# Moving query projections, statistics, roots and the meta rows in a hybrid encoder layer

## The chip, the cores and the metric

The kernel runs on one core of a Trainium2 chip. Such a core has five engines, each with a queue of its own that it works through in order: TensorE (PE in the rows: matrix products and transposes into PSUM banks; PEld is its weight load), VectorE (DVE), ScalarE (ACT), GpSimd (POOL) and SyncE (SP, which here issues the DMA transfers). The metric is the device time of one execution in microseconds, as the median of three runs.

## The reference, cut to what matters

```python
def encoder_layer(h, ...):
    u = rms_norm(h, pre_g)                       # 16 meta rows + 512 or 1024 tokens, 1024 wide
    z = u @ w_in                                 # 1024 x 7168
    c_val, c_glu, c_gate, q, k, v, a_gate = split(z)
    conv_out = conv_module(c_val, c_glu, ...) * silu(c_gate)
    att = neighbourhood_attention(q, k, v, ...) * silu(a_gate)
    y = concatenate([conv_out, att]) @ w_out
    return h + rms_norm(y, post_g)

def conv_module(val, glu_gate, conv_w, conv_b, ln_g, ln_b):
    u = val * sigmoid(glu_gate)
    y = depthwise_conv(u, conv_w) + conv_b       # 31 taps
    return silu(layer_norm(y, ln_g, ln_b))
```

Attention has 16 heads of 64; each query sees a window of 8 rows by 16 columns of a grid 64 wide, with a relative bias, and the 16 meta tokens. Prompt and samples share the meta tokens, so that all 16 + 512 + 1024 columns go through one program.

## The kernel before

All projections are computed nearly in full precision by splitting each fp32 operand into a high part of type f32r and an f32r rest. A product is then three f32r products: high by high, high by low, low by high. `split_w` (L140) makes the two parts of a weight: ScalarE copies the high part, and VectorE or GpSimd subtracts it from the raw weight. `proj` (L175) is one projection tile: 8 slices of 128 rows by 3 products, 24 in all, of up to 512 columns.

The program has four parts.

1. **Start**, 0 to about 36 us. `prenorm(s)` normalizes tile `s` (0 is the 16 meta rows, 1 to 12 are 128 tokens each), transposes it and splits it into `uh` and `ul`. The loop at L363 takes them in the order 1, 0, 2, 3, ... and puts the first units of `v_units` (24 products of 256 columns, one for each token tile) between them. `load_v(0)` loads and splits the first quarter of the value weights into `vh` and `vl`; its low part is made by VectorE, those of later quarters by GpSimd. At step `IVM` the value products of the meta rows are issued (`v_meta`, with the small fp32 product with `sel`, L305).
2. **Convolution**, to about 640 us: projections on TensorE beside 31 taps for each channel block on VectorE. The results go to DRAM (`zs`).
3. **Attention**, about 648 to 1163 us: 8 pairs of heads, each with 3 groups of queries in 2 halves, 48 steps in all. A step `n` of the loop at L682 issues the scores of half `n` (`scores`: 4 tiles `ss`, each three f32r products, then the maximum on VectorE, L584, the exponential on ScalarE, and a scaling), the weighted sums of half `n-2` (`weighted`, L615, plain fp32), the transposes of half `n-1` (`transposes`, L599, and ScalarE's copy `pT`, L601), and two kinds of filling work:
   - `between(p, i)`, with `i` from 0 to 5 within a pair: the query projections `pair_q` (its own groups 1 and 2 at `i` 0 and 2, the next pair's group 0 at `i` 5) and the four key projections of the next pair (two at `i` 1, one each at 3 and 4). `pair_q` ends in four copies `qh` on ScalarE and four subtractions `ql` on VectorE, `pair_proj` in `kh` and `kl`.
   - one step of the generator `statistics`: layer-norm moments of the convolution's result, read back from `zs`. For each of 12 token tiles it loads two half tiles, sums over the channel blocks on VectorE (L659, into `ms`, a part of the tile `cw_sb`), sums over the partitions by an fp32 product with `ones` on TensorE (L663), and stores the row to `std`; then the same for the squared deviations. These are 24 `ones` products. Its last two steps (L671 to L676) read all variances back, take the root on ScalarE and the reciprocal on VectorE, and store the result.
4. **Output**, about 1196 us to the end: `mix(t)` builds one token tile (L763 to L770: subtract the mean, multiply, Silu, multiply with the gate, split) and `product` multiplies it with the output weights (L790). The first tile's convolution part, `mix(0, (0,))`, is placed behind the last transposes copy and ahead of the weight loads `load_wo`. The last two gate projections (`a_gate(6, 7)`) run on TensorE from 1163 to 1196 us.

PSUM has three banks for projections and `ones` products, two for scores, two for transposes and one for weighted sums. Three query buffers are used in turn, one for a half.

The order of the source is not the final order. A scheduler of the framework orders each engine's queue when the program is built, and it may bring an instruction forward past others if its inputs allow. `tc.issue_after(x)` holds the instructions of its block that run on the engine of `x` behind `x`; `last_qk`, `last_mm`, `last_pv` and `last_pt` are the latest score product, projection product, weighted sum and transposes copy.

Of the kernel before, what the change touches and what calls it, by code (L numbers as in the profile page):

```python
# [16 lines left out]
DC = 8  # L17
# [25 lines left out]
NVS = 7  # L43
NXT = 4
LAG = 1
IVM = 3
TAP_US = 2.3
STAT0 = 3
STEP_US = dict(v=2.8, c=5.5, a=5.5)
# [44 lines left out]
def tile_encoder(ctx: ExitStack, tc: tile.TileContext, mt, xn, w_main, w_v, wo, cw, cb, lg, lb, pg, postg, rbt, rmask, y):  # L94
    nc = tc.nc
# [77 lines left out]
    last_mm = [None]  # L173
# [112 lines left out]
    def load_v(qv):  # L286
        raws, his, los = [], [], []
        for half in range(2):
            raws.append(wpool.tile([128, 4, 256], F32, name="wraw", tag="wraw", bufs=2))
            nc.sync.dma_start(raws[half], w_v[qv][:, half * 4:half * 4 + 4])  # L290
            his.append(vpool.tile([128, 4, 256], F32R, name="vh", bufs=2))
            los.append(vpool.tile([128, 4, 256], F32R, name="vl", bufs=2))
            split_w(raws[half], his[half], los[half], nc.vector if qv == 0 else nc.gpsimd)
        return raws, his, los

    def v_meta(qv, raws):
# [16 lines left out]
    def v_units():  # L313
        for qv in range(4):
            _, vh, vl = vws.pop(qv)
            for t in range(12):
                ps = new_mm()
                uh, ul = u_cols(16 + 128 * t, 16 + 128 * t + 128)
                for dc in range(DC):
                    for i, (u, w) in enumerate(((uh, vh), (uh, vl), (ul, vh))):  # L320
                        nc.tensor.matmul(ps[:, :256], lhsT=u[dc // 4][:, dc % 4, :], rhs=w[dc // 4][:, dc % 4, :],  # L321
                                         start=(dc == 0 and i == 0), stop=(dc == DC - 1 and i == 2))
                vs = vpool.tile([128, 256], F32, name="vs", bufs=3)
                nc.scalar.copy(out=vs, in_=ps[:, :256])  # L324
                row = (ROW_P, ROW_A, ROW_B)[t // 4]
                for i in range(2):
                    nc.sync.dma_start(vd[(t % 4) * 2 + i, row * 8:row * 8 + 64, qv * 256:qv * 256 + 256], vs[i * 64:i * 64 + 64])
                if t == 11 and qv < 3:
                    vws[qv + 1] = load_v(qv + 1)
                    metas.append(qv + 1)  # L330
                yield
# [28 lines left out]
        nc.gpsimd.tensor_tensor(out=sel, in0=sel, in1=ident[:, j:j + 16], op=ALU.add)  # L360
    with tc.tile_pool(name="start", bufs=2, side="right", reuse_waits="tile") as sp:
        gb = sp.tile([128, D], F32, name="gb", bufs=1)
        for i, s in enumerate((1, 0) + tuple(range(2, 13))):  # L363
            prenorm(s, sp, gb)
            if i == 0:
                vws[0] = load_v(0)
                vraw0 = vws[0][0]
            if i == IVM:
                v_meta(0, vraw0)
            if LAG <= i < LAG + NVS:  # L370
                next(vfill)
            if s == 5:
                ahead[8] = load_w(8)
                ahead[0] = load_w(0)
        for dst, src in ((cw_sb[:, :, :KW], cw), (cb_sb, cb), (lg_sb, lg), (lb_sb, lb), (rm_sb, rmask)):
            nc.sync.dma_start(dst, src)
# [36 lines left out]
    for c in range(8):  # L413
        if c > 0:
            z = new_z()
        steps = convolve(c, z)
# [65 lines left out]
    last_qk = [None]  # L482
# [145 lines left out]
    def between(p, i):  # L628

        if i in (0, 2):  # L630
            pair_q(p, i // 2 + 1)
        elif p == NPAIR - 1:
            for _ in range(1 if i == 1 else 2):
                next(rest)
        elif i == 5:
            pair_q(p + 1, 0)
        else:
            if i == 1:
                knext[0] = pair_proj(p + 1)
                next(knext[0])  # L640
            next(knext[0])
# [5 lines left out]
    def statistics():  # L647
        for t in range(TG // 128):
# [8 lines left out]
            for moment in range(2):  # L657
                for x, sl in hx:
                    nc.vector.tensor_reduce(out=ms[:, sl], in_=x.rearrange("p c t -> p t c"), op=ALU.add, axis=mybir.AxisListType.X)  # L659
                yield  # L660
                ps = new_mm()
                with tc.issue_after(last_qk[0].ins):
                    nc.tensor.matmul(ps[:, :128], lhsT=ones, rhs=ms, start=True, stop=True)  # L663
                nc.scalar.copy(out=row[0:1], in_=ps[0:1, :128])
                nc.sync.dma_start(std[moment:moment + 1, tsl], row[0:1])
                if moment == 0:
                    for x, sl in hx:
                        nc.vector.tensor_tensor(out=x, in0=x, in1=ps[:, sl].unsqueeze(1).broadcast_to([128, 8, 64]), op=ALU.subtract)
                        nc.scalar.activation(out=x, in_=x, func=AF.Square)
        yield  # L670
        s = std[1:2]  # L671
        var = bass.AP(s.tensor, s.offset, [[1, 128], [128, TG // 128]])
        nc.sync.dma_start(rv, var)
        nc.scalar.activation(out=rv, in_=rv, func=AF.Sqrt, bias=eps_sb[:, 1:2])
        nc.vector.reciprocal(rv, rv)
        nc.sync.dma_start(var, rv)  # L676
        yield

    stats = statistics()
    knext, last_pv, last_pt = [None], [None], [None]  # L680
# [2 lines left out]
    for n in range(len(groups) + 2):  # L683
        if n < len(groups):
            p, g, hf = groups[n]
# [9 lines left out]
            next(rest)  # L695
        if 0 <= n - 1 < len(groups):
            transposes(*groups[n - 1])
        if n >= STAT0:
            next(stats, None)
        if n < len(groups):  # L700
            between(p, g * 2 + hf)
    with tc.issue_after(last_pv[0]):
        for _ in a_gate(6, 7):
            pass
# [65 lines left out]
            (nc.vector if t < MLT else nc.gpsimd).tensor_tensor(out=ml, in0=mx, in1=mh.bitcast(F32), op=ALU.subtract)  # L770

    with tc.issue_after(last_pt[0]):
        mix(0, (0,))
    for n in range(16):
        if n == 6:
# [132 lines left out]
```

## Time and profile before

| | before |
|---|---|
| median of 3 runs | 1474.44 us (1472.86 to 1474.65) |
| the profiled execution | 1473.84 us, of which 1471.8 us are its span (first to last instruction) |
| TensorE busy | 1442.7 us, 98% of the span |
| VectorE, ScalarE, GpSimd busy | 1012.5, 559.5, 250.2 us |
| share of TensorE in the chain that ended last | 86% |

An engine is busy while it executes an instruction; waiting for a semaphore is idle time. "The chain that ended last" follows the program back from its last instruction to whatever released each step. In the rows, an instruction's length includes the time it takes to pass through the engine, and the next one starts before it ends; the pace of products is therefore read from start to start. A bracket at a row's end gives the idle time just before it and what ended that. A line such as L495 is that of the kernel before; after the change, lines beyond L317 are one or two higher.

### The profile page before, as it was taken

The numbers are of one execution on the slowest core, as the hardware profiler recorded it, in microseconds if no ns is written. First come the engines' busy times: TensorE is split into PE (matmuls) and PEld (weight loads), VectorE is DVE, ScalarE is ACT, GpSimd is POOL, SyncE is SP. The second block draws the span as 40 slices with busy tenths as digits, with TensorE's granted clock in tenths as the row PEclk, the third lists the DMA queues.
The fourth block names the chain that finished last, engine by engine and source line by source line (L and its number), as shares of the span: only waits on it lengthen the run. The fifth ranks groups of instructions, "written<-read, shape, count | busy, mean of one in ns | idle before, by whom it ended". The sixth has DMA issues, their size and how long they took to land.

```text
span 1471.8 us, 24149 instructions
## 1 busy us (share of the span) xinstructions
PE 1442.7 (98%) x9536; PEld 1237.9 (84%) x9536; DVE 1012.5 (69%) x1741; ACT 559.5 (38%) x1299; POOL 250.2 (17%) x186
## 2 busy tenths in 40 slices
PE   7999999999999999999999999999999999999998
PEld 6988998988998888888888888888878878888886
DVE  6599999998999899846767676666654174432421
ACT  7312111112111111235545555455544475554440
POOL 2042022112101211222111121111110102122120
PEclk9999999999999999999999999999999999999999
DMA  8113113312231212343132232322232495644531
GB/s 272 35 47 114 50 55 110 93 40 88 82 91 50 99 48 87 108 101 102 43 94 79 76 93 59 102 79 77 46 101 74 150 304 148 173 132 137 159 106 43
DMA packets 153465, 145.21 MB, mean 99 GB/s; under 512 B 37216, under 2 KB 125432, under 8 KB 153352
## 3 DMA queue, kind: packets, MB, share of 16 engines
q1 hardware_dynamic: 153352, 143.67, 32.7%
q8 instruction: 75, 1.23, 0.3%
q14 instruction: 38, 0.31, 0.1%
HBM read 105.35 MB, written 42.72 MB: 101 GB/s over the span
## 4 chain that ended last, share of the span: by engine, by line
PE 86%; issue 4%; DMA 4%; DVE 2%; ACT 2%; POOL 1%; SPq 0%; DVEq 0%; POOLq 0%; ACTq 0%
PE mm L180 35%; PE py L790 17%; PE tp L180 9%; PE ss L577 5%; PE po L180 5%; PE po L615 4%; PE mm L321 3%; PE tp L599 3%; PE tp L321 3%; DMA wraw<-in_w_main 1%; DMA wraw<-in_wo 1%; POOL vl L142 1%; PE po L321 1%; PE mm L663 1%; DMA wraw<-in_w_v 1%
## 5 line engine op out<-in xcount | busy, mean ns | idle before, releaser
L180 PE MATMUL mm<-uw,whi 128*128 128x512 f32 (+2 forms) x1904 | 566.3, 372 | 0.0
L272 DVE SCALAR_TENSOR_TENSOR z<-ub,cw_sb,z 128x1536 f32<-128x1536 f32 (+2 forms) x270 | 497.4, 1849 | 8.1
L180 PEld LDWEIGHTS mm<-uw,whi 128*128 128x128 f32 x1904 | 343.7, 188 | 56.9 <-issue 1.3
L180 PE MATMUL mm<-uw,wlo 128*128 128x512 f32 (+2 forms) x952 | 353.3, 371 | 1.1 <-POOL wlo L142 1.1
L142 POOL TENSOR_TENSOR wlo<-wraw,whi 128x1024 fp32r<-128x1024 f32 x48 | 130.5, 2719 | 627.7 <-ACT whi L141 618.5
L180 PEld LDWEIGHTS mm<-uw,wlo 128*128 128x128 f32 x952 | 179.3, 188 | 26.5 <-POOL wlo L142 1.4
L790 PE MATMUL py<-uw,mh 128*128 128x512 f32 x576 | 181.0, 395 | 0.0
L180 PE MATMUL tp<-uw,whi 128*128 128x512 f32 (+2 forms) x512 | 132.9, 344 | 0.0
L790 PEld LDWEIGHTS py<-uw,mh 128*128 128x128 f32 x576 | 108.1, 188 | 25.4
L588 ACT ACTIVATE pt<-pt,sm 128x216 f32<-128x216 f32 (+4 forms) x192 | 96.8, 505 | 54.5 <-DVE sm L587 53.4
L584 DVE CUSTOM_DVE_ANT_0 pt<-ss,ei 128x216 f32<-128x216 f32 (+2 forms) x144 | 62.1, 436 | 77.7 <-PE ss L577 66.2
L790 PE MATMUL py<-uw,ml 128*128 128x512 f32 x288 | 113.4, 394 | 0.0
L601 ACT COPY pT<-tp 108x256 f32<-108x256 f32 (+4 forms) x192 | 76.9, 420 | 70.0 <-PE tp L599 62.8
L180 PEld LDWEIGHTS tp<-uw,whi 128*128 128x128 f32 x512 | 89.3, 188 | 11.6
L763 DVE TENSOR_TENSOR mx<-mx,mb 128x1024 f32<-128x1024 f32 x12 | 14.7, 1225 | 115.6 <-DMA mx<-zs 115.6
L180 PE MATMUL tp<-uw,wlo 128*128 128x512 f32 (+2 forms) x256 | 88.1, 344 | 0.0
L321 PE MATMUL mm<-vh,uw 128*128 128x256 f32 x448 | 84.2, 285 | 1.4 <-ACT vs L324 0.7
L770 POOL TENSOR_TENSOR ml<-mx,mh 128x1024 fp32r<-128x1024 f32 x20 | 48.2, 2430 | 205.9 <-ACT mh L769 205.9
L590 DVE TENSOR_SCALAR pt<-pt,sm 128x216 f32<-128x216 f32 (+4 forms) x192 | 78.3, 411 | 3.8
L599 PE MATMUL tp<-ident,pt 128*96 128x128 f32 (+2 forms) x480 | 78.2, 273 | 0.4 <-ACT pT L601 0.4
L141 ACT CAST whi<-wraw 128x1024 fp32r<-128x1024 f32 x48 | 50.3, 1049 | 62.7 <-DMA wraw<-in_w_main 21.0
L180 PE MATMUL po<-uw,whi 128*128 128x512 f32 (+2 forms) x272 | 73.2, 348 | 0.0
(171 smaller groups left out, 2164.2 us busy)
## 6 DMA issues: line engine op xcount, KB each, us to landing
wraw<-in_w_main SPq DMA_DIRECT2D x48, 512.0 KB
xt<-in_xn SPq DMA_DIRECT2D x12, 512.0 KB
vd<-vs SPq DMA_DIRECT2D x96, 64.0 KB
zs<-zc SPq DMA_DIRECT2D x24, 256.0 KB
cgd<-ag SPq DMA_DIRECT2D x24, 256.0 KB
agd<-ag SPq DMA_DIRECT2D x24, 256.0 KB
ag<-zs SPq DMA_DIRECT2D x24, 256.0 KB
mad<-mo SPq DMA_DIRECT2D x24, 256.0 KB
```

What stands on the lines that cost most here:

```text
L142: eng.tensor_tensor(out=lo, in0=raw, in1=hi.bitcast(F32), op=ALU.subtract)
L180: last_mm[0] = nc.tensor.matmul(ps[:, :n], lhsT=w[:, dc, :], rhs=u[dc // 4][:, dc % 4, :], start=(dc == 0 and i == 0), stop=(dc == DC - 1 ...
L272: nc.vector.scalar_tensor_tensor(out=zv, in0=ub[:, a:b, k:k + 512], scalar=cw_sb[:, c, k:k + 1], in1=zv, op0=ALU.mult, op1=ALU.add)
L321: nc.tensor.matmul(ps[:, :256], lhsT=u[dc // 4][:, dc % 4, :], rhs=w[dc // 4][:, dc % 4, :], start=(dc == 0 and i == 0), stop=(dc == DC - ...
L577: last_qk[0] = nc.tensor.matmul(ss[:, :nk * w], lhsT=q[:, jj].rearrange("p h x -> p (h x)"), rhs=k[:, b0:b0 + nk, ra:ra + rn, :].rearrange ...
L584: nc.vector.tensor_tensor_reduce(out=pv.rearrange("p (k x) -> p k x", k=nk), in0=sv_, in1=e.rearrange("p k r c -> p k (r c)"), scale=1.0, ...
L588: last[0] = nc.scalar.activation(out=pv, in_=pv, func=AF.Exp, bias=sm[:, 1:2], scale=1.0, accum_out=sm[:, 2:3])
L590: nc.vector.tensor_scalar(out=pv, in0=pv, scalar1=sm[:, 3:4], scalar2=None, op0=ALU.mult)
L599: nc.tensor.transpose(out=tp[:kt, k * 128:k * 128 + 128], in_=pv[:, k * kt:k * kt + kt], identity=ident)
L601: last_pt[0] = nc.scalar.copy(out=pT[:kt, :nt * 128], in_=tp[:kt, :nt * 128]).ins
L615: last_pv[0] = nc.tensor.matmul(po[hs, j, :], lhsT=v, rhs=pT[:kt, k * 128 + h * 64:k * 128 + h * 64 + 64], start=(k == 0), stop=(k == nt - ...
L790: nc.tensor.matmul(pss[hf], lhsT=m[e // 8][:, e % 8], rhs=w[e][:, hf * 512:hf * 512 + 512], start=(n == 0 and i == 0), stop=(n == 15 and i ...
```

## The change

Five edits:

- the meta rows are normalized fourth instead of second, and their value products are issued one step later (`IVM`);
- the low part of the first value weights is made by GpSimd instead of VectorE, and the first value unit's 24 products are ordered by kind (8 high by high, 8 with the weights' low part, 8 with the tokens' low part);
- the next pair's first query projection is issued at `i` 4 instead of 5, and the last key projection at 5 instead of 4;
- a step of `statistics` comes behind `between` instead of ahead of it, and its `ones` product is held behind the last projection product instead of the last score product;
- the root and the reciprocal of the variances leave `statistics` and become `roots()`, called with the first `mix` behind the last transposes copy.

```diff
-IVM = 3
+IVM = 4
...
-            split_w(raws[half], his[half], los[half], nc.vector if qv == 0 else nc.gpsimd)
+            split_w(raws[half], his[half], los[half])
...
-                for dc in range(DC):
-                    for i, (u, w) in enumerate(((uh, vh), (uh, vl), (ul, vh))):
-                        nc.tensor.matmul(ps[:, :256], lhsT=u[dc // 4][:, dc % 4, :], rhs=w[dc // 4][:, dc % 4, :],
-                                         start=(dc == 0 and i == 0), stop=(dc == DC - 1 and i == 2))
+                parts = list(enumerate(((uh, vh), (uh, vl), (ul, vh))))
+                steps = [(dc, x) for dc in range(DC) for x in parts] if qv or t else [(dc, x) for x in parts for dc in range(DC)]
+                for dc, (i, (u, w)) in steps:
+                    nc.tensor.matmul(ps[:, :256], lhsT=u[dc // 4][:, dc % 4, :], rhs=w[dc // 4][:, dc % 4, :],
+                                     start=(dc == 0 and i == 0), stop=(dc == DC - 1 and i == 2))
...
-        for i, s in enumerate((1, 0) + tuple(range(2, 13))):
+        for i, s in enumerate((1, 2, 3, 0) + tuple(range(4, 13))):
...
-        elif i == 5:
+        elif i == 4:
             pair_q(p + 1, 0)
...
-                with tc.issue_after(last_qk[0].ins):
+                with tc.issue_after(last_mm[0]):
                     nc.tensor.matmul(ps[:, :128], lhsT=ones, rhs=ms, start=True, stop=True)
...
-        yield
+
+    def roots():
         s = std[1:2]
         var = bass.AP(s.tensor, s.offset, [[1, 128], [128, TG // 128]])
         nc.sync.dma_start(rv, var)
         nc.scalar.activation(out=rv, in_=rv, func=AF.Sqrt, bias=eps_sb[:, 1:2])
         nc.vector.reciprocal(rv, rv)
         nc.sync.dma_start(var, rv)
-        yield
...
+        if n < len(groups):
+            between(p, g * 2 + hf)
         if n >= STAT0:
             next(stats, None)
-        if n < len(groups):
-            between(p, g * 2 + hf)
...
     with tc.issue_after(last_pt[0]):
+        roots()
         mix(0, (0,))
```

The built programs show where the instructions stand. First the boundary between two pairs on TensorE's queue. In the rows of before, `mm_6074` is the projection of the next pair's first queries, whose copies are `qh0` and `ql0`, and `ss_6127` is the first score of that pair.

```order
L180 MATMUL mm_6074<-uw_110,whi_5548 128x512
L180 MATMUL mm_6074<-uw_110,wlo_5549 128x512
L180 MATMUL mm_6074<-uw_112,whi_5548 128x512
L599 MATMUL tp_6194<-ident_92,pt_5970 104x128 x3
L599 MATMUL tp_6200<-ident_92,pt_5981 104x128 x3
L577 MATMUL ss_6127<-kh_5552,qh0_5180 128x264
L577 MATMUL ss_6127<-kl_5553,qh0_5180 128x264
L577 MATMUL ss_6138<-kh_5552,qh0_5180 128x264
L577 MATMUL ss_6138<-kl_5553,qh0_5180 128x264
L577 MATMUL ss_6127<-kh_5552,ql0_5181 128x264
```

After the change the same projection is `mm_6760`. It ends here, with the last key projection (`mm_6887`) and transposes behind it:

```order
L180 MATMUL mm_6760<-uw_110,whi_6349 128x512
L180 MATMUL mm_6760<-uw_110,wlo_6350 128x512
L180 MATMUL mm_6760<-uw_112,whi_6349 128x512
L180 MATMUL mm_6887<-uw_117,whi_5939 128x512
L180 MATMUL mm_6887<-uw_117,wlo_5940 128x512
L600 MATMUL tp_6604<-ident_92,pt_6421 96x128 x2
```

and the first scores of the pair, `ss_6944`, stand here, behind the other key projections, the next query projection and the first tile's keys of the pair after (`mm_7172`):

```order
L616 MATMUL po_6708<-pT_6735,vt_6415 64x64 x6
L616 MATMUL po_6708<-pT_6741,vt_6415 64x64 x6
L616 MATMUL po_6708<-pT_6747,vt_6415 64x64 x6
L616 MATMUL po_6708<-pT_6752,vt_6415 64x64 x4
L578 MATMUL ss_6944<-kh_6353,qh0_5180 128x264
L578 MATMUL ss_6944<-kl_6354,qh0_5180 128x264
L578 MATMUL ss_6944<-kh_6353,ql0_5181 128x264
L578 MATMUL ss_6955<-kh_6353,qh0_5180 128x264
L578 MATMUL ss_6955<-kl_6354,qh0_5180 128x264
L600 MATMUL tp_6875<-ident_92,pt_6690 104x128 x3
L578 MATMUL ss_6955<-kh_6353,ql0_5181 128x264
L180 MATMUL mm_7172<-uw_109,wlo_6757 128x272
```

Before, six transposes lie between the query projection's end and the first score, and the scores follow each other directly. After, there are two whole projections and part of a third, and weighted sums, transposes and projection products lie among the scores.

The second place is a `ones` product on TensorE's queue. Before, it (`mm_6058`) stands between weighted sums and a projection, at all 24:

```order
L615 MATMUL po_5891<-pT_5930,vt_5612 64x64 x6
L615 MATMUL po_5891<-pT_5935,vt_5612 64x64 x4
L663 MATMUL mm_6058<-cw_sb_95,ones_87 128x128
L180 MATMUL mm_6074<-uw_109,whi_5548 128x512
L180 MATMUL mm_6074<-uw_109,wlo_5549 128x512
L180 MATMUL mm_6074<-uw_111,whi_5548 128x512
```

After the change (`mm_7067`) it stands directly behind a projection product:

```order
L578 MATMUL ss_6817<-kh_5552,ql2_5357 128x312
L180 MATMUL mm_7034<-uw_114,wlo_6350 128x512
L180 MATMUL mm_7034<-uw_116,whi_6349 128x512
L664 MATMUL mm_7067<-cw_sb_95,ones_87 128x128
L180 MATMUL mm_7172<-uw_109,whi_6756 128x272
L180 MATMUL mm_7172<-uw_109,wlo_6757 128x272
```

Of the 24, 20 now stand behind a projection product, 3 behind a score and 1 behind a transpose; a projection product follows 8 of them, a transpose 9 and a score 7. Weighted sums hand over directly to transposes at 27 places instead of 4.

The third place is ScalarE's queue around the root. Before, it stands in the attention, ahead of key copies (L477) and the exponentials (L588):

```order
L495 ACTIVATE qh_5356<-mm 64x4x64
L601 COPY pT<-tp 96x384 x2
L674 ACT_TABLE_LOAD
L674 ACTIVATE rv<-rv,eps_sb 128x12
L477 CAST kh<-mm 128x8x64
L588 ACT_TABLE_LOAD
L588 ACTIVATE pt,sm<-pt,sm 128x208
```

After, it stands behind the last transposes copy, ahead of the gate's Silu (L768), the copies of the first output weights (L745) and the mix's Silu (L767):

```order
L602 COPY pT<-tp 104x256
L676 ACT_TABLE_LOAD
L676 ACTIVATE rv<-rv,eps_sb 128x12
L768 ACT_TABLE_LOAD
L768 ACTIVATE gt<-gt 128x1024
L745 CAST woh_12184<-wraw 128x1024
L745 CAST woh_12190<-wraw 128x1024
L342 COPY ag<-mm 128x512
L767 ACTIVATE mx<-mx,lb_sb,lg_sb 128x128 x8
```

The table loads went from the middle of the attention to its end.

## Rows read from the trace of the kernel before

**Rows 1.** Busy time by window: length, each engine's us, granted clock, DMA share.
```profile
640.00:1165.00 525.00, 514.57 (x4484) 441.31 (x4483) 321.33 (x1195) 273.54 (x798) 76.83 (x84) 1.00 0.28 76
```

**Rows 2.** TensorE's waits, 640 to 1165 us: us in total, times, longest.
```profile
PE ss L577 <- ACT qh L495: 6.6, 7, 2.5
PE ss L577 <- DVE sm L584: 3.1, 7, 0.5
PE tp L599 <- ACT pT L601: 0.4, 1, 0.4
PE ss L577 <- DVE ql L496: 0.2, 1, 0.2
```

**Rows 3.** Timeline of TensorE at a pair boundary: start us, length us.
```profile
759.95 0.82 PE L599 MATMUL tp<-ident,pt 128*104 128x128 f32 x6
761.44 0.39 PE L577 MATMUL ss<-kh,qh 128*128 128x264 f32 x1 [0.67 <-ACT qh L495]
...
762.92 0.39 PE L577 MATMUL ss<-kh,qh 128*128 128x264 f32 x1 [0.47 <-DVE sm L584]
```

**Rows 4.** Timeline of ScalarE at the same boundary.
```profile
760.15 0.38 ACT L495 ACTIVATE qh<-mm 64x256 fp32r<-64x256 f32 x1 [0.85 <-PE mm L180]
761.01 0.38 ACT L495 ACTIVATE qh<-mm 64x256 fp32r<-64x256 f32 x1 [0.48 <-DVE ql L496]
```

**Rows 5.** Timelines of VectorE and TensorE at the seventh boundary.
```profile
1075.77 1.23 DVE L763 TENSOR_TENSOR mx<-mx,mb 128x1024 f32<-128x1024 f32 x1 [4.61 <-DMA mx<-zs]
...
1077.85 0.39 PE L577 MATMUL ss<-kh,qh 128*128 128x264 f32 x1 [2.52 <-ACT qh L495]
```

**Rows 6.** Timelines: the root on ScalarE, the mix's Silu, TensorE's first output product.
```profile
1052.91 0.31 ACT L674 ACTIVATE rv<-rv,eps_sb 128x12 f32<-128x12 f32 x1 [3.48 <-DMA rv<-std]
...
1162.94 3.20 ACT L766 ACTIVATE mx<-mx,lb_sb,lg_sb 128x128 f32<-128x128 f32 x8
...
1196.17 0.39 PE L790 MATMUL py<-woh,mh 128*128 128x512 f32 x1
```

**Rows 7.** Timeline of TensorE: weighted sums without and with a ones product.
```profile
745.04 1.50 PE L615 MATMUL po<-pT,vt 96*64 96x64 f32 x44
...
746.82 0.40 PE L180 MATMUL mm<-uw,wlo 128*128 128x512 f32 x1
...
751.96 1.50 PE L615 MATMUL po<-pT,vt 96*64 96x64 f32 x44
753.39 0.49 PE L663 MATMUL mm<-cw_sb,ones 128*128 128x128 f32 x2
...
753.95 0.40 PE L180 MATMUL mm<-uw,wlo 128*128 128x512 f32 x1
```

**Rows 8.** Timeline of TensorE: the sel product (L305) between projection products.
```profile
227.10 0.39 PE L180 MATMUL mm<-uw,whi 128*128 128x512 f32 x1
227.41 0.61 PE L305 MATMUL mm<-vs,sel 128*16 128x256 f32 x2
227.95 0.50 PE L180 MATMUL mm<-uw,whi 128*128 128x512 f32 x1
228.29 0.39 PE L180 MATMUL mm<-uw,wlo 128*128 128x512 f32 x1
```

**Rows 9.** Timeline of TensorE: transposes between projection products.
```profile
756.52 0.40 PE L180 MATMUL mm<-uw,whi 128*128 128x512 f32 x1
...
757.22 0.49 PE L599 MATMUL tp<-ident,pt 128*104 128x128 f32 x3
...
757.77 0.39 PE L180 MATMUL mm<-uw,wlo 128*128 128x512 f32 x1
```

**Rows 10.** Timelines of VectorE and GpSimd at the start.
```profile
8.95 1.23 DVE L142 TENSOR_TENSOR vl<-wraw,vh 128x1024 fp32r<-128x1024 f32 x1 [0.99 <-ACT vh L141]
...
27.60 5.70 POOL L142 TENSOR_TENSOR wlo<-wraw,whi 128x1024 fp32r<-128x1024 f32 x2 [24.98 <-ACT whi L141]
...
28.00 3.04 DVE L196 SCALAR_TENSOR_TENSOR un<-xt,rs,gb 128x1024 f32<-128x1024 f32 x1
```

## The prediction

> **What bounds the kernel now.** I read the windows first. Over the attention part (640 to 1165 us), TensorE is busy for 514.6 of 525 us at a granted clock of 1.00 [rows 1]. So the kernel is bound by TensorE, which is nearly always at work. Its time can change in two ways only: an idle gap closes or opens, or the same products stream at another pace.
>
> The table of waits for the same stretch names the gaps [rows 2]: 10.3 us in 16 waits, 9.7 of it in 14 waits of score products (`ss`). Of these, seven wait for ScalarE's copy `qh` of the queries and seven for VectorE's softmax step L584. The timeline shows the place [rows 3]. At a pair boundary the transposes end, the first score waits 0.67 us for `qh`, and 1.5 us after it another waits 0.47 us for L584. The same two waits stand at six of the seven boundaries.
>
> The reason is visible in ScalarE's timeline [rows 4]: the copies of one query projection (four `qh`, each followed by VectorE's `ql`) start only when the projection has ended, and each waits for the `ql` before it: 0.86 us from one to the next, 3.4 us for the four. The projection of the next pair's first queries is the last thing ahead of the first scores, so its copies are in plain sight. The scores then come four in a row with nothing between, faster than L584 empties their two banks: hence the second wait.
>
> At the seventh boundary the first score waits 2.52 us [rows 5]. There VectorE stood 4.61 us in L763, the first step of the output mix, waiting for a load. Everything behind it on VectorE's queue stood too, `ql` among it, and ScalarE's next `qh` behind that.
>
> **The change part by part.** *Queries one group sooner.* In the new order some 17 us of TensorE work lies between the end of the query projection and the first score that reads it (24 products of 512 columns for the keys, 24 for the next queries, and what stands between; 0.23 us a piece, a third of 756.52 to 757.22 in [rows 9]), and the copies take 3.4. So the `qh` waits go. The scores of a boundary no longer come in a row either, but with weighted sums, transposes and projection products between, so the L584 waits go with them, and so do the three single waits, which come from the same crowding.
>
> A gap costs more than its wait. From 757.22 to 757.77 lie three transposes and one product [rows 9]: 0.55 less 0.23 leaves 0.11 us for each transpose. So after the six at 759.95 the next product could have started at 760.61. It started at 761.44, 0.83 us later, where the wait is given as 0.67. The difference of 0.16 us is overlap that every stop loses. The term is 10.3 + 16 × 0.16 = **-12.9 us**. Its bounds are 0 (the waits come back elsewhere; a rival) and -12.9.
>
> *Roots behind attention.* The table load of the square root, the root, and the mix's load and VectorE step leave the attention; the 2.52 us above are already in the sum. They now stand behind ScalarE's last transposes copy, at about 1162 us, and must be done when the first output product starts, at 1196.17 [rows 6]. The chain is: read the variances 3.5 us [the wait in rows 6], root 0.3, store and reload some 7 (two more transfers of that kind, an estimate), two VectorE steps of 1.23 [rows 5], eight Silu 3.2 [rows 6]. That is 17 us, so it ends near 1180. The cover is the last gate projections, which fill TensorE up to 1196; 16 us are left. SyncE issues the store and the reload ahead of loads of output weights, which shifts these by 2 to 3 us. **0**; bounds -1 and +3, should a late weight reach TensorE.
>
> *Statistics behind projections.* 24 products with `ones` change neighbours. This is the one cost that I see. They are fp32 and run as two passes, while all projections and scores are f32r. Today every one stands directly behind weighted sums, which are fp32 themselves. From the first weighted sum to the second projection product takes 1.78 us without a `ones` product and 1.99 us with it [rows 7]: 0.21 us, its bare streaming. Moved, 20 of 24 stand behind an f32r projection, 3 behind scores, 1 behind transposes. Before's trace has such a neighbourhood for a product of the same kind, the `sel` product L305 [rows 8]: from the projection product before it to the second one behind it, 1.19 us. Two products of 0.23 and two passes of twice the columns (0.42) account for 0.88; 0.31 us are left, of which 0.11 is the slow start of the next projection product (227.95 to 228.29).
>
> So a moved product costs between 0 and 0.31 us more. I take 0.31 for the 8 that a projection follows, and 0.22 for the 16 that transposes or scores follow, where that slow start may not be paid: 2.5 + 3.5 = **+6.0 us**; bounds 0 and +7.4. Transposes are fp32 too, and as many columns as a pass of `ones`, but between projection products each takes 0.11 us [rows 9], no more than a bare pass (0.21 / 2). So the new order's scattering of transposes among products is set at nothing.
>
> The Trainium skill ("TensorE: Matmul & The Clock Gate", § Wait — 56ns, not 53.3ns?) gives the start-to-start time of a warm product as its columns over 2.4 GHz plus about 2.5 ns, and names no price for a change of kind. By that rule this term is 0 and the time some 6 us lower; [rows 8] do not agree with it, as far as one form shows.
>
> *Start.* VectorE loses two splits of 1.23 us, of which [rows 10] show the first, and the meta rows' normalization comes two tiles later, so the next tiles' rows can be ready up to 2.5 us sooner. Against that, GpSimd takes 2.85 us for a split (5.70 for two) [rows 10], and the first unit needs both. The reordering (eight products that need no low part go first) covers some of that. While GpSimd runs a split, a normalization on VectorE took 3.04 us [rows 10], against the 1.23 of an operation of that size: +1.8 if one meets it. I take **-0.5**; bounds -2.5 and +2.5.
>
> The Trainium skill ("SBUF — State Buffer", § Who interferes with whom) says that a VectorE instruction with two SBUF inputs and a GpSimd one that reads SBUF exclude each other. The 3.04 us agree. By that rule the move of the split would cost about 2 us instead of saving 0.5.
>
> *Sum:* -12.9 + 6.0 - 0.5 = -7.4. Against the profiled execution's 1473.84 this is 1466.4. The median of the runs is 0.6 above that execution: **1467.0**.
>
> **The rivals.** *No price for changed neighbours* (chance 0.11). For it: transposes show none [rows 9]. Against it: [rows 8]. Then -13.4, 1461.0.
>
> *Other waits take the place of those removed* (0.20). The last key projection now falls next to the boundary, the three projection banks are used again sooner, and copies of keys and queries meet on VectorE and ScalarE. For it: VectorE is busy 61% of the stretch [rows 1] and one late operation holds up its queue, as at the seventh boundary. Against it: in before, of many reuses, only the boundary ones wait. If a third to all of the 12.9 come back: 1471.3 to 1479.9, mostly below 1476.
>
> *Slower: the `ones` product waits for its sums* (0.13). Place: the 24 `ones` products. They used to stand behind the scores and weighted sums; now they are held only behind the last projection, which can end before VectorE's two column sums of the group have run. Then TensorE stops in the middle of its queue, with scores and transposes behind. In before none of them waits [rows 2]. The price is the lateness per product; from 7.4 / 24 = 0.31 us on, the gain is gone, from 0.43 us it is slower than the bound below. At 0.5 us each: +12, 1479. For it: each sum is two reductions behind whatever VectorE has in its queue. Against it: by the new order and [rows 9], 7 us of TensorE work or more lie between one moment's product and the next.
>
> **How the numbers follow.** The forecast (0.56) spans 1463 to 1470.5. About 0.2%, or 3 us, is what a measurement can tell from no change: faster is below 1471.5, slower above 1477.4. The forecast, the no-price case and 0.03 of the new waits are faster: 0.70. The rest of the new waits is the same: 0.17. The third rival is slower: 0.13. The range from 1461.0 to 1475.5 leaves out the slower rival, the part of new waits above it, and part of the no-price case.
>
> **What the changed profile would show.** Right: no `qh` or L584 wait of a score at the boundaries; between 640 and 1165 us about 1 us of idle; a first projection product behind the `ones` product that starts late, about 0.5 us per moved `ones` product in all; no table load at 1048; root and mix done by 1185 and the first output product without a wait. Wrong: `ones` products that wait for the sums of L660; score or projection products that wait for `kl`, `ql` or `pT`; `ones` products at 0.21 us; a first output product that waits for the mix; a first unit that ends later than 16 us without the second starting sooner than 18.

## The result and the profile after

| | before | after |
|---|---|---|
| median | 1474.12 us (4 runs) | 1466.37 us (1465.41 to 1466.88, 4 runs) |
| ratio to before | | 0.9948, 95% interval 0.9934 to 0.9963 |
| span of the profiled execution | 1471.8 us | 1464.5 us |
| mean granted TensorE clock | 0.999 | 0.996 |

The time lies within 1 us of the forecast, but not by the forecast's sum. The profile after is read here in the order in which the forecast read that of before. First the windows and the table of TensorE's waits from 640 to 1165 us; after the change attention ends earlier, so part of the output stage lies in this stretch. The columns are those of [rows 1, 2]; the second window is one of ten microseconds in the output stage.

```profile
640.00:1165.00 525.00, 520.91 (x4552) 452.66 (x4551) 327.66 (x1197) 280.01 (x801) 77.24 (x82) 1.00 0.30 82
...
1180.00:1190.00 10.00, 8.55 (x30) 6.86 (x31) 7.12 (x7) 7.89 (x10) 0.00 (x0) 0.83 0.85 283
PE mm L180 <- ACT ag L342: 3.3, 1, 3.3
PE po L616 <- ACT pT L602: 0.5, 1, 0.5
PE tp L600 <- ACT pT L602: 0.2, 1, 0.2
```

The waits for `qh` and for L584 of [rows 2] are gone, all fourteen. What has come is a wait of 3.3 us of a projection product (L180) for `ag`, ScalarE's copy of a finished gate tile, and in the second window a clock of 0.83.

How long did attention take? The tile views give the first and last start of each group. Before, first the scores (first at 648.1 us), then the weighted sums (last at 1162.9):

```profile
L577 PE MATMUL ss<-kh,qh x192: 277/304/416, 648.1 to 1139.3; 128*128 128x264 f32 x64, 128*128 128x288 f32 x48, 128*128 128x312 f32 x48, 128*128 128x256 f32 x32
...
L615 PE MATMUL po<-pT,vt x1408: 221/222/272, 684.9 to 1162.9; 96*64 96x64 f32 x88, 104*64 104x64 f32 x88
```

and after:

```profile
L578 PE MATMUL ss<-kh,qh x192: 278/365/417, 647.0 to 1125.9; 128*128 128x264 f32 x64, 128*128 128x288 f32 x48, 128*128 128x312 f32 x48, 128*128 128x256 f32 x32
...
L616 PE MATMUL po<-pT,vt x1408: 222/222/271, 688.8 to 1142.7; 96*64 96x64 f32 x88, 104*64 104x64 f32 x88
```

From the first score to the last weighted sum it was 514.8 us and is 495.7. That is **-19.1 us**, where the whole span lost only 7.3. From the last weighted sum to the end it was 308.9 us and is 321.8: **+12.9 us**. The start, up to the first score, makes up the rest, -1.1 us.

At the pair boundary that answers to [rows 3, 4], the timelines of ScalarE and TensorE show the copies `qh` of the first half some 20 us before the score that reads them. Two scores then follow each other:

```profile
739.61 0.36 ACT L496 ACTIVATE qh<-mm 64x256 fp32r<-64x256 f32 x1
...
741.08 0.38 ACT L496 ACTIVATE qh<-mm 64x256 fp32r<-64x256 f32 x1
...
760.55 0.39 PE L578 MATMUL ss<-kh,qh 128*128 128x264 f32 x1
...
761.02 0.28 PE L578 MATMUL ss<-kh,qh 128*128 128x264 f32 x1
```

Next a `ones` product that has moved, on TensorE's timeline. It answers to [rows 7, 8]:

```profile
757.01 0.39 PE L180 MATMUL mm<-uw,whi 128*128 128x512 f32 x1
757.24 0.38 PE L664 MATMUL mm<-cw_sb,ones 128*128 128x128 f32 x2
757.38 0.37 PE L180 MATMUL mm<-uw,whi 128*128 128x272 f32 x1
757.59 0.29 PE L180 MATMUL mm<-uw,wlo 128*128 128x272 f32 x1
```

From the projection product before it (757.01) to the second one behind it (757.59) it is 0.58 us. One product of 512 columns takes 0.23 of it and one of 272 some 0.13 (757.72, the next start, less 757.59 in the same timeline). The two passes cost 0.22 us, and at the seven other places that a projection follows 0.22 or 0.23. Forecast were 0.52 at such a place; behind weighted sums it was 0.21 [rows 7].

Now the loss. The waits of TensorE behind the last weighted sum, of which before had one of 0.9 us:

```profile
PE py L792 <- ACT mh L770: 4.6, 1, 4.6
PE mm L180 <- ACT ag L342: 3.3, 1, 3.3
PE py L792 <- ACT ag L342: 1.8, 1, 1.8
```

SyncE's queue shows where they begin. The store of the roots is issued at 1144.28, and the reload of the moments (`mb`, L752), which needs that store to have landed, at 1154.83: 10.5 us later. SyncE works through its queue in order, so the loads of the output weights stand behind the reload. The first line is from the list of its waits, 1130 to 1165 us; it puts 9.3 us on the store:

```profile
SPq L752 <- DMA std<-rv: 9.3, 1, 9.3
...
1144.28 0.37 SPq L678 DMA_DIRECT2D std<-rv  x1
...
1154.83 0.37 SPq L752 DMA_DIRECT2D mb<-std  x1
1155.29 0.42 SPq L735 DMA_DIRECT2D wraw<-in_wo  x1
```

On VectorE, ScalarE and TensorE:

```profile
1160.17 1.23 DVE L764 TENSOR_TENSOR mx<-mx,mb 128x1024 f32<-128x1024 f32 x1 [15.34 <-DMA mb<-std]
...
1161.38 1.05 ACT L745 CAST woh<-wraw 128x1024 fp32r<-128x1024 f32 x1 [14.08 <-DMA wraw<-in_wo]
1162.34 0.58 ACT L342 COPY ag<-mm 128x512 f32<-128x512 f32 x1
...
1159.29 0.39 PE L180 MATMUL mm<-uw,whi 128*128 128x512 f32 x1
1162.97 0.50 PE L180 MATMUL mm<-uw,whi 128*128 128x512 f32 x1 [3.29 <-ACT ag L342]
```

VectorE waits 15.34 us for the reload, which lands 5.3 us after its issue. ScalarE waits 14.08 us for an output weight, and on its queue the copy of a finished gate tile (1162.34) stands behind that weight's copy. So a projection bank stays full, and TensorE waits 3.29 us until 1162.97. In the forecast this chain was to run beside the last gate projections and be covered by them; all of it is some 20 us sooner here, as attention ends sooner. But the gate projections need those very queues and were held up with the rest.

A stop can cost more than itself. Behind that of 4.6 us the output products come 0.43 us apart instead of 0.23, the lower of the clock's two levels (1.2 GHz; the granted clock from 1201.52 to 1205.95 is 0.50):

```profile
1201.52 0.80 PE L792 MATMUL py<-woh,mh 128*128 128x512 f32 x1 [4.56 <-ACT mh L770]
1202.11 0.63 PE L792 MATMUL py<-wol,mh 128*128 128x512 f32 x1
1202.54 0.63 PE L792 MATMUL py<-woh,mh 128*128 128x512 f32 x1
```

The three stops are 9.7 us; the slow products cost 1.7 us more behind that of 1.8 us and 2.1 behind that of 4.6. Less the 0.9 us of before, this makes 12.6 of the 12.9.

Last the start, which answers to [rows 10]: GpSimd's two splits, the normalization that VectorE runs beside them, and TensorE's wait in the first unit.

```profile
9.03 4.70 POOL L142 TENSOR_TENSOR vl<-wraw,vh 128x1024 fp32r<-128x1024 f32 x2 [6.41 <-ACT vh L141]
...
12.96 1.85 DVE L196 SCALAR_TENSOR_TENSOR un<-xt,rs,gb 128x1024 f32<-128x1024 f32 x1
...
13.79 0.74 PE L322 MATMUL mm<-vl,uw 128*128 128x256 f32 x4 [1.16 <-POOL vl L142]
```

### The profile page after: what moved, and what is told of

It reads as the page before. It is cut to its first block, busy times and chain, and to the rows that moved or that the text cites. A ratio compares the mean times of both kernels' runs of the same rounds, so it can differ in the third digit from the quotient of the medians.

```text
span 1464.5 us, 24133 instructions
## 1 busy us (share of the span) xinstructions
PE 1436.8 (98%) x9536; PEld 1238.6 (85%) x9536; DVE 1014.2 (69%) x1739; ACT 562.7 (38%) x1298; POOL 256.6 (18%) x188
## 4 chain that ended last, share of the span: by engine, by line
PE 92%; DMA 3%; ACT 2%; DVE 1%; POOL 1%; issue 1%; SPq 0%; DVEq 0%; ACTq 0%; POOLq 0%
PE mm L180 37%; PE py L792 18%; PE tp L180 9%; PE mm L322 5%; PE ss L578 5%; PE po L180 5%; PE po L616 4%; PE tp L600 4%; PE tp L322 3%; PE po L322 1%; POOL vl L142 1%; DMA std<-rv 1%; DMA yo<-in_wo 0%; ACT mx L767 0%; DMA wraw<-in_wo 0%
## 5 line engine op out<-in xcount | busy, mean ns | idle before, releaser
L180 PE MATMUL mm<-uw,whi 128*128 128x512 f32 (+2 forms) x1904 | 560.1, 371 | 3.3 <-ACT ag L342 3.3
L180 PEld LDWEIGHTS mm<-uw,whi 128*128 128x128 f32 x1904 | 341.8, 188 | 59.2 <-ACT ag L342 4.3
L180 PE MATMUL mm<-uw,wlo 128*128 128x512 f32 (+2 forms) x952 | 352.4, 370 | 1.1 <-POOL wlo L142 1.1
L180 PEld LDWEIGHTS mm<-uw,wlo 128*128 128x128 f32 x952 | 179.0, 188 | 27.2 <-POOL wlo L142 1.4
L180 PE MATMUL tp<-uw,whi 128*128 128x512 f32 (+2 forms) x512 | 132.9, 344 | 0.0
L180 PEld LDWEIGHTS tp<-uw,whi 128*128 128x128 f32 x512 | 89.3, 188 | 11.6
L180 PE MATMUL tp<-uw,wlo 128*128 128x512 f32 (+2 forms) x256 | 88.1, 344 | 0.0
L600 PE MATMUL tp<-ident,pt 128*96 128x128 f32 (+2 forms) x480 | 85.5, 275 | 0.3 <-ACT pT L602 0.2
L591 DVE TENSOR_SCALAR pt<-pt,sm 128x216 f32<-128x216 f32 (+4 forms) x192 | 72.1, 375 | 4.9
L180 PE MATMUL po<-uw,whi 128*128 128x512 f32 (+2 forms) x272 | 72.9, 347 | 0.0
```

The source lines that it names most:

```text
L180: last_mm[0] = nc.tensor.matmul(ps[:, :n], lhsT=w[:, dc, :], rhs=u[dc // 4][:, dc % 4, :], start=(dc == 0 and i == 0), stop=(dc == DC - 1 ...
L591: nc.vector.tensor_scalar(out=pv, in0=pv, scalar1=sm[:, 3:4], scalar2=None, op0=ALU.mult)
L600: nc.tensor.transpose(out=tp[:kt, k * 128:k * 128 + 128], in_=pv[:, k * kt:k * kt + kt], identity=ident)
```

## The experiments

For each run three stretches of its profiled execution are given, read as above: up to the first score, from there to the last weighted sum, and from there to the end of the span. They add up to the span. The ratio is to the kernel before on the same chip, with its 95% interval.

| run | median us | ratio | first score | attention | rest |
|---|---|---|---|---|---|
| before | 1474.12 | | 648.1 | 514.8 | 308.9 |
| after | 1466.37 | 0.9948 (0.9934 to 0.9963) | 647.0 | 495.7 | 321.8 |
| 1 after, roots in statistics | 1453.56 | 0.9867 (0.9850 to 0.9884) | 648.1 | 496.3 | 307.9 |
| 2 after, statistics as before | 1467.27 | 0.9959 (0.9944 to 0.9975) | 648.0 | 497.3 | 320.4 |
| 3 after, queries at `i` 5 | 1466.38 | 0.9954 (0.9939 to 0.9969) | 647.9 | 494.5 | 322.0 |
| 4 after, start as before | 1466.25 | 0.9953 (0.9938 to 0.9968) | 647.6 | 495.7 | 321.4 |
| 5 before, queries at `i` 4 | 1457.11 | 0.9903 (0.9886 to 0.9921) | 646.6 | 499.1 | 308.8 |
| 6 before, statistics as after | 1452.58 | 0.9871 (0.9857 to 0.9886) | 646.0 | 495.3 | 309.1 |
| 7 before, roots as after | 1483.46 | 1.0074 (1.0059 to 1.0089) | 648.2 | 511.0 | 322.7 |
| 8 after, roots by rows | 1458.48 | 0.9903 (0.9886 to 0.9919) | 647.2 | 495.7 | 313.4 |
| 9 before, the hold alone | 1455.34 | 0.9875 (0.9858 to 0.9891) | 646.2 | 499.0 | 308.1 |
| 10 before, the order alone | 1456.94 | 0.9887 (0.9872 to 0.9901) | 647.5 | 498.4 | 309.2 |
| 11 before, statistics and start as after | 1453.55 | 0.9863 (0.9848 to 0.9878) | 647.2 | 495.0 | 309.0 |

**1. The roots back in `statistics`.**

```diff
-    def roots():
+        yield
         s = std[1:2]
...
         nc.sync.dma_start(var, rv)
+        yield
...
-        roots()
         mix(0, (0,))
```

> The changed kernel with the roots back at the end of statistics, all else as changed. Theory A (from the two traces): behind the last transposes the root's store and the reload of the moments take some 16 us together and hold up SyncE's loads of output weights; that made TensorE lose 12.9 us after the last weighted sum. Put back, these go: about 1454 us, up to 1457 if VectorE's early mix step costs the 2.7 us again that it cost at the seventh boundary. Theory B (as predicted: the roots behind attention are covered by the last gate projections): nothing to win there, 1466 to 1469 us.

1453.56 us, 12.8 below the changed kernel, and the rest of the span is 307.9 us instead of 321.8. On SyncE's queue the store is now issued at 1034.53 and the reload at 1058.42, in the middle of attention, where no output weight stands behind them:

```profile
1034.53 0.37 SPq L677 DMA_DIRECT2D std<-rv  x1
...
1058.42 0.37 SPq L752 DMA_DIRECT2D mb<-std  x1
```

Of TensorE's waits from 1130 us on, one of 0.5 us is left, for a transposes copy. Attention stays at 496.3 us, though the first mix step is back in it. Theory A holds: the place of the roots cost the changed kernel all it lost.

**2. The statistics as before, all else as after.**

```diff
-                with tc.issue_after(last_mm[0]):
+                with tc.issue_after(last_qk[0].ins):
...
-        if n < len(groups):
-            between(p, g * 2 + hf)
         if n >= STAT0:
             next(stats, None)
+        if n < len(groups):
+            between(p, g * 2 + hf)
```

> The changed kernel with statistics ahead of between again and its ones products held behind the last score product. Theory A: a ones product costs 0.22 us in either place, and the new order only saves slow hand-overs from weighted sums to projections: 1.5 to 3 us slower, 1468 to 1469.5 us. Theory B (as predicted): a ones product between f32r products costs 0.25 us more than behind weighted sums, so undoing it wins 6 us: 1460.5 us.

1467.27 us, a little under Theory A's range, and attention is 1.6 us longer than in the changed kernel. So `ones` products between f32r products cost no more than behind weighted sums, and the forecast's +6.0 us has the wrong size: it is about 0. The boundary waits are nearly gone here too, from 640 us to the end of attention:

```profile
PE ss L578 <- DVE sm L585: 0.4, 1, 0.4
PE tp L600 <- ACT pT L602: 0.4, 1, 0.4
```

**3. The queries at `i` 5 again, all else as after.**

```diff
-        elif i == 4:
+        elif i == 5:
             pair_q(p + 1, 0)
```

> The changed kernel with the next pair's first query projection at i 5 again and the last key projection at 4. Theory A: the waits at the pair boundaries come back with their full price as start-to-start times show it, some 14 to 16 us: 1480 to 1482 us. Theory B (the predicted price): 12.9 us, 1479 us. Rival: the spacing comes from statistics behind between, and the place of the query projection matters little: under 1472 us.

1466.38 us, and attention is the shortest of all with 494.5 us. Theory A falls: not one `qh` or L584 wait came back. TensorE's only wait from 640 us to the end of attention:

```profile
PE po L616 <- ACT pT L602: 0.3, 1, 0.3
```

The timelines of ScalarE and TensorE show why. The source puts the next pair's first query projection last again, but the scheduler brings it forward all the same. Its last product starts at 746.88 and ends at 747.27; the two copies `qh` that the pair's first score reads follow, and the second ends at 748.96; this score starts at 761.24, 14.0 us behind the projection's end. At the seven boundaries it is 14.0 to 17.6 us. Then come projection products, and the next scores, not in a row.

```profile
746.88 0.39 PE L180 MATMUL mm<-uw,whi 128*128 128x512 f32 x1
...
747.31 0.38 ACT L496 ACTIVATE qh<-mm 64x256 fp32r<-64x256 f32 x1
...
748.58 0.38 ACT L496 ACTIVATE qh<-mm 64x256 fp32r<-64x256 f32 x1
...
761.24 0.37 PE L578 MATMUL ss<-kh,qh 128*128 128x264 f32 x1
...
764.65 0.37 PE L578 MATMUL ss<-kh,qh 128*128 128x264 f32 x1
```

So the place of the query projection in the source doesn't set its place on the queue, and this run doesn't speak against the forecast's mechanism, that the copies must be done ahead of the score.

What is left to test is a third reading: before, the boundary was bad by one tight order (projection, six transposes, four scores in a row), and any edit that loosens it clears the waits. Runs 5, 6, 9 and 10 test that.

**4. The start as before, all else as after.** Undone are `IVM`, the order of the tiles, the engine of the split and the order of the first unit.

> The changed kernel with the start as before (meta rows second, low part on VectorE, first unit by slices). Theory A: the first score comes 1.1 us earlier by the traces, and all of it reaches the end: 1467.5 us. Rival: GpSimd's split costs the first unit what the earlier tiles win, and the 1.1 us come from elsewhere: 1466.4 us. Both lie within what a run can tell; the trace's time of the first score decides (647.0 as changed, 648.1 before).

1466.25 us, the first score at 647.6. Over all runs the first score lies between 646.0 and 648.2 with the start of before, and between 647.0 and 648.1 with the new one. The 1.1 us are no more than the spread between executions; the new start's worth can't be told from 0.

**5. Only the queries at `i` 4, on the kernel before.** The diff is that of run 3 with its signs turned.

> The kernel before with the query projection at i 4 and the last key projection at 5, nothing else. Theory A2 (either move alone clears the boundary waits): attention from the first score to the last weighted sum near 497 us as in the run with the old statistics, against 514.8 before; the mix of the first tile may still hold up VectorE once: 1454 to 1458 us. Theory B (both moves are needed, or the waits go only part of the way): above 1463 us.

1457.11 us; attention 499.1 us, 15.7 less than before. The rest of the span is as before, 308.8. TensorE's waits from 640 us to the end of attention:

```profile
PE tp L599 <- ACT pT L601: 1.8, 2, 1.4
PE ss L577 <- DVE sm L584: 0.4, 1, 0.4
```

**6. Only the statistics as after, on the kernel before.** The diff is that of run 2 with its signs turned.

> The kernel before with statistics behind between and its ones products held behind the last projection product, nothing else; the query projection stays the last of a pair. Theory A2: attention near 494.5 us as in the run with the queries at i 5, 1453 to 1457 us. Theory B (the query move is what clears the waits): no less than 1470 us, and the qh waits stand.

1452.58 us; attention 495.3 us. With the query projection still the last of its pair in the source, no `qh` wait is left. Either edit alone clears the boundary; both together gain 18.5 us in attention (run 1; 19.1 with the roots moved too), not the sum of 15.7 and 19.5.

**7. Only the roots as after, on the kernel before.** The diff is that of run 1 with its signs turned.

> The kernel before with the roots behind attention, nothing else. Theory A: the seventh boundary's waits shrink from 2.7 to 1.1 us, and what follows the last weighted sum takes 10 to 13 us longer, as in the changed kernel: 1482 to 1485 us. Theory B (the tail cost in the changed kernel comes from attention ending sooner, not from the roots): 1472 us.

1483.46 us, slower than before. The rest of the span is 13.8 us longer, and attention 3.8 shorter: the mix no longer holds up VectorE at the seventh boundary, and the `qh` wait of 2.5 us there is gone. TensorE's longest waits from 640 us to the end show both:

```profile
PE py L791 <- ACT mh L769: 6.0, 1, 6.0
PE mm L180 <- ACT ag L341: 4.1, 1, 4.1
PE ss L577 <- ACT qh L495: 4.0, 6, 0.7
PE ss L577 <- DVE sm L584: 3.1, 7, 0.5
```

**8. The roots behind attention, but by rows.** The variances are held as 12 rows of 128 values in the freed tile `ms`, so that the store moves 12 pieces of 512 bytes instead of 1536 of 4. The place in the source stays.

```diff
-        var = bass.AP(s.tensor, s.offset, [[1, 128], [128, TG // 128]])
+        var = bass.AP(s.tensor, s.offset, [[128, TG // 128], [1, 128]])
+        rv = ms[:TG // 128]
...
-        nc.scalar.activation(out=rv, in_=rv, func=AF.Sqrt, bias=eps_sb[:, 1:2])
+        nc.scalar.activation(out=rv, in_=rv, func=AF.Sqrt, bias=eps_sb[:TG // 128, 1:2])
```

> The changed kernel with the variances held as 12 rows of 128 instead of 128 rows of 12, so that the read and the store in roots move 12 pieces of 512 bytes and not 1536 of 4; the place of the roots is as changed. Theory A3 (the slow landing of the 1536 small pieces, 10.5 us in the trace, is what makes the chain long): the store lands in 2 to 3 us, SyncE goes on 8 us sooner, and 7 to 10 of the 12.9 us come back: 1456 to 1459 us. Rival (the chain's length is in the other steps and in SyncE's order): 1464 to 1467 us.

1458.48 us; of the 12.9 us of the rest of the span 8.4 come back. SyncE issues the reload 1.45 us after the store, not 10.5, and its list of waits has none for the store:

```profile
1145.35 0.32 SPq L679 DMA_DIRECT2D std<-cw_sb  x1
...
1146.32 0.38 SPq L736 DMA_DIRECT2D wraw<-in_wo  x1
1146.80 0.40 SPq L753 DMA_DIRECT2D mb<-std  x1
```

One output weight's load has also moved ahead of the reload, so the run doesn't part the shorter store from that. The rest of the span is still 4.5 us longer than before. Of the three stops one is left, 3.9 us for the second tile's `mh`; the ten products behind it take 3.9 us instead of 2.3, at a granted clock of 0.59. Why this `mh` is late, no run takes apart.

**9 and 10. The hold alone, and the order alone, on the kernel before.**

```diff
-                with tc.issue_after(last_qk[0].ins):
+                with tc.issue_after(last_mm[0]):
```

> The kernel before with one line changed: the ones products are held behind the last projection product instead of the last score product; statistics stays ahead of between, queries at i 5, start and roots as before. Theory H (the hold sets the spacing: free of the last score, the products let scores, transposes and projection products mix): attention near 496 us and no boundary waits, 1453 to 1457 us. Theory O (the place of the step in the source sets it): attention near 514 us, 1472 to 1475 us.

1455.34 us, attention 499.0 us; no `qh` wait is left. In run 10 the hold is as before and only the step stands behind `between`:

```diff
-        if n >= STAT0:
-            next(stats, None)
         if n < len(groups):
             between(p, g * 2 + hf)
+        if n >= STAT0:
+            next(stats, None)
```

> The kernel before with the statistics step behind between, its ones products still held behind the last score product; all else as before. Theory H: the boundary waits stay, 1468 to 1474 us. Theory O: they go, 1453 to 1458 us.

1456.94 us, attention 498.4 us; TensorE's waits from 640 us to the end of attention:

```profile
PE tp L599 <- ACT pT L601: 2.0, 4, 0.8
PE ss L577 <- DVE sm L584: 0.8, 2, 0.7
```

Both do it, so neither theory excludes the other, as with the queries: three small edits, each alone, take 15.7 to 16.4 us out of attention. The third reading holds, and the timelines show what these runs share. Before, the copies for a pair's first score ended 0.05 us ahead of it, with TensorE waiting. In runs 3, 5, 6 and 9 they end 7 to 24 us ahead. In run 10 it is 1.0 us at five of the seven boundaries, with 2.3 us from the projection's end to the score, and that is enough:

```profile
752.90 0.40 PE L180 MATMUL mm<-uw,whi 128*128 128x512 f32 x1
...
754.20 0.38 ACT L495 ACTIVATE qh<-mm 64x256 fp32r<-64x256 f32 x1 [0.48 <-DVE ql L496]
...
755.60 0.37 PE L577 MATMUL ss<-kh,qh 128*128 128x264 f32 x1
```

Why the scheduler orders the queue so after each edit, no run shows.

**11. The statistics and the start as after, queries and roots as before.**

> The kernel before with the statistics and the start as changed, but queries at i 5 and roots in statistics as before. If the new start is worth the 1.1 us by which the first score came earlier: 1451.5 us. If that was a difference between executions: 1452.6 us, as with the statistics alone. The point is the best version of the edits; the start alone may stay below what can be told.

1453.55 us, where the statistics alone gave 1452.58. The intervals of the ratios overlap for the most part, so the start is worth nothing that shows. Runs 1, 6 and 11 are the best versions, 1.3 to 1.4% under the kernel before and, by the medians, 13 to 14 us under the changed one.

## Why the prediction held, point by point

The time was right and the direction was right, but three of the four terms were wrong. The waits gave 4.6 us more than forecast and the `ones` products cost 7.6 less, while the roots cost 12.9 that stood at nothing. That these cancel almost fully is luck.

| term | forecast | measured | by |
|---|---|---|---|
| waits at the boundaries and the three single ones | -12.9 | -15.7 to -17.5 | attention against before: run 5 (queries alone), run 2 (roots out of attention too, as in the forecast's term) |
| `ones` products and hand-overs | +6.0 | -1.6 to -2.8 | attention: after against run 2, run 1 against run 5 |
| roots behind attention | 0 | +12.9 | the rest of the span; +12.8 by the medians of after and run 1 |
| start | -0.5 | can't be told from 0 | runs 4 and 11 |
| total | -7.4 | -7.3 | spans |

*The boundary waits* went, as forecast, and the price was somewhat larger. The timeline of [rows 3] shows what the overlap of 0.16 us left out. It goes on, before, with

```profile
764.10 1.50 PE L615 MATMUL po<-pT,vt 104*64 104x64 f32 x44
```

From the transposes at 759.95 to these weighted sums six transposes and twelve scores take 4.15 us, and their streaming is about 2.1. So a boundary lost 2.0 us, of which the waits' table lists 1.1; a first product behind a stop comes 0.23 us before the next, twice the pace of its 264 columns, and a pause of 0.15 us stands in no list. The mechanism held: the waits went because the copies were done ahead of the score. But *the gain was put on one edit, and two others give it as well*. The forecast's step "in the new order some 17 us of TensorE work lies between" is true (20 to 36 us from the projection's end to the score after the change), but it doesn't need this edit, since run 3 has 14.0 to 17.6 us without it, and not that much, since run 10 has 2.3 us at five boundaries and no `qh` wait. And since each of three edits does it alone, the gain of the change is not the sum of gains of its parts.

*The `ones` term* failed at "before's trace has such a neighbourhood for a product of the same kind, the `sel` product". It is of the same kind but not of the same form (16 weight columns, 256 moving ones), and its 0.31 us did not carry over: the moved `ones` product costs 0.22 us. The row that was nearer, [rows 7], had the right price. The Trainium skill ("TensorE: Matmul & The Clock Gate", § Wait — 56ns, not 53.3ns?) names no price for a change of kind, and the `ones` products agree with it in that (0.22 us against 0.21); why `sel` takes longer, no run shows. The small gain may lie in the hand-overs, as weighted sums are followed by a transpose or a score at 45 places in attention now instead of 9; no run tests that.

*The roots* failed at two steps. "Store and reload some 7" was 15.9 us (10.5 and 5.3): the estimate took a read's wait for the length of a store of 1536 pieces of 4 bytes and of a reload that depends on it. And "shifts these by 2 to 3 us" left out that SyncE stands still until the store has landed, with every later load behind it; the first stop came from there and through ScalarE's queue. The first tile's mix itself ended by 1171, when gate projections still ran on TensorE (the last product starts at 1179.27). With the shorter store of run 8 two of the three stops are gone and 8.4 of the 12.9 us; the third stop stays, and its cause is open. Run 7 shows that this costs 13.8 us on the kernel before as well, so it is not an effect of attention ending sooner.

*The start:* the normalization beside GpSimd's splits took 1.85 us instead of the 1.29 of the next one (14.93 in the same timeline), and the first unit waited 1.16 us for a split. Both are of the kind that the forecast feared, the first with 0.56 us instead of its 1.8; the gain that it set against them doesn't show in the time of the first score. The Trainium skill ("SBUF — State Buffer", § Who interferes with whom) has the two engines shut each other out for such operands; the trace agrees in that the operation took longer while a split ran.

*The rivals.* The case of no price for changed neighbours (chance 0.11) was right in its mechanism: of the signs of being wrong, `ones` products at 0.21 us came. Its time of 1461.0 was not, because of the roots. New waits in place of the old ones did come, but in the output stage, not at the boundary. No `ones` product waited for its sums, so the slower rival had no part. Of the signs of being right, the first output product without a wait failed: it waited 1.8 us.

## What to carry to other kernels

A stall at a seam of a tight schedule can have several sufficient cures, and undoing an edit in the source need not undo its effect on the queue: read the place of an instruction from the trace. Test each edit alone before adding up gains, and undo them one at a time, since a harmful one can hide behind a good one. Here the change gained 19.1 us and gave back 12.9, and leaving out a single edit takes the kernel from 0.5% to 1.3% under the one before.

When a small transfer is moved behind the main work, ask what stands behind it on the issuing engine's queue, and time a store by its pieces, not its bytes: 6 KB in 1536 pieces held the queue 10.5 us.

## What the runs showed of the hardware that was not expected

The store of 6 KB in pieces of 4 bytes let the dependent reload go only after 10.5 us; in 12 pieces of 512 bytes it was 1.45 us (1145.35 to 1146.80 in run 8), with another load issued in between. SyncE waited for the first store for 9.3 us and for the second not at all. And behind two of TensorE's three stops in the output stage, those of 1.8 and 4.6 us, products came 0.43 us apart until 1185.4 and 1206.0, at the lower clock (granted 0.59 from 1181.45 to 1185.66 and 0.50 from 1201.52 to 1205.95), which cost 1.7 and 2.1 us beyond the stop; behind that of 3.3 us they came at 0.23 (granted 1.00 from 1162.97 to 1168).
